# Bias table in one transfer, broadcast rows in stretches of 2 KB, and the last output bank in two halves

## The chip, the cores and the metric

The kernel runs on one core of a Trainium2 chip. The metric is the device time of one execution in microseconds (us), the median of several runs. The engines are named as in the profile: PE (matrix engine; PEld is its weight load, which runs beside the matmuls), DVE (vector), ACT (scalar), POOL, and SP, whose queue issues most of the transfers. ACT issues some as well. Each engine works through its own queue in order.

## The reference

A backbone of two layers over 256 latent tokens of width 2048, with 256 context tokens. Each layer begins with a modulated RMS norm; shift, scale and gate come from a conditioning vector by a matrix-vector product.

```python
for i in range(DEPTH):                       # DEPTH = 2
    shift, scale, gate = adaln(c, ada_w[i], ada_b[i])       # silu(c) @ w + b
    h = modulate(rms_norm(x, norm_g[i]), shift[:, None], scale[:, None])
    ...
    if i % 2 == 0:
        y, yc = na_ssd_mixer(h, hc, ...)     # 16 attention heads beside 32 SSD heads, then @ w_out
    else:
        y = short_conv_mixer(h, ...)         # four projections, a convolution of 3 taps, a gate, @ sc_w_out
    x = x + gate[:, None] * y
```

Two pieces of the first layer matter here. The attention of a latent row adds a bias, looked up in a small table for each head, to the scores of the latent keys, and masks the keys outside a window:

```python
s_lat = einsum('bqhd,bkhd->bhqk', qr, kb) * scale + bias      # bias = rpb[:, dr_idx, dc_idx]
s_lat = where(mask, s_lat, -inf)
s_ctx = einsum('bqhd,bkhd->bhqk', qr, k_ctx) * scale
pr = softmax(concatenate([s_lat, s_ctx]))
```

The SSD heads, in both directions of the sequence, use the running sum of dt * a along the sequence, and its exponential:

```python
cs = cumsum(dtc * a, axis=1)
decay = exp(where(tri, cs[:, :, None] - cs[:, None, :], -inf))
y = y + einsum('bign,bgrpn->bigrp', cc, h) * exp(cs)[..., None]
```

## The kernel before

All products with weights run in a form that keeps most of fp32: each operand is split into a high part and the rest, and three matmuls (high x high, high x low, low x high) add into one PSUM bank. A weight chunk of 512 KB is loaded by SP into one of five raw buffers; ACT casts it to the high part (line 422); DVE subtracts to get the low part (line 429); then PE uses both. The chunks go through in a fixed order (first layer's inputs, four groups of attention and SSD projections, w_out, then sc_in and sc_out of the second layer), and this stream sets the time line.

Everything else is written into the gaps by a planner. `Plan` holds a modelled clock for each engine and a modelled landing time for each transfer (`RATE`, 270 bytes a ns, line 42; lines 110 to 118). Small generators ("tasks") hold the side work. Between matmuls `pump` asks `may` for each task whether its next step is due on the modelled clocks, and if so writes it out there. So the order of instructions on each engine is fixed when the program is built, and a changed cost or condition in the plan can move other instructions. There are three lists of tasks: urgent, side and back; a task of the last is taken only when the first two have nothing due.

The tasks that the change touches:

- `gemv_gen` (line 872), the only task of the last list: the gate of the first layer and all of the second layer's modulation are 128 dot products on DVE, each of a loaded block of 128 x 1024 with the conditioning vector (line 885). Their loads (`adaT`) share the raw buffers with the weights: `issue` (line 367) loads the next block only when a buffer is free and enough weight chunks are already there. The results are asked for in three stages by `n_back` (lines 1725, 1762, 2103).
- `head_gen` (line 1134), one of 16 attention heads: it loads the head's bias into one of two bias tiles (line 1141), adds the mask to three pieces of it (line 1146), and later reads the tile as the bias of the 416 keys of each of two query blocks (line 1163). Between the pieces the tile holds zeros, set once by a memset (line 994), for the context keys.
- `dt_gen` (line 1264): it computes the running sums and writes them, and their exponentials, to DRAM as `csr` and `exr`, 64 rows of 256 (32 heads, twice for the two directions), by ACT's queue (lines 1352, 1353).
- `make_x` and `group_gen`: each head's two rows are read back, spread over 64 or 128 partitions, in stretches of 1 KB (lines 1482 and 1523).
- `fin_gen` (line 2101): the last step for each 512 output columns. It loads the gate's row, multiplies the bank with it on DVE (line 2112), adds the residual (line 2114) and sends the result out (line 2116). For the last 512 columns the final matmuls are ordered by rows of tokens: all that is left for the first 128 tokens (t = 0), then the same for the second (lines 2129 to 2139), so that the first half's end runs under the second half's matmuls.

Of the kernel before, what the change touches and what calls it, by code (L numbers as in the profile page):

```python
# [11 lines left out]
ALU = mybir.AluOpType  # L12
# [129 lines left out]
def kernel(ctx: ExitStack, tc, x, cx, ada0, w0, adaT, w_in, w_out, sc_in, sc_out, rpb, small, const,  # L142
# [9 lines left out]
    plan = Plan()  # L152
# [5 lines left out]
    def drt(shape, name):  # L158
        return dr.tile(list(shape), F32, name="dram_" + name)
# [35 lines left out]
    def mm(o, l, r, start, stop):  # L195
        E(T.matmul(o, l, r, start=start, stop=stop, skip_group_check=True))  # L196
# [143 lines left out]
    def give(pool, *bs):  # L340
        pool.extend(bs)
# [501 lines left out]
    def dot_gen():  # L843
# [8 lines left out]
        for j in DOTS:  # L852
# [17 lines left out]
            got.add(("S", j))  # L870

    def gemv_gen():
        yield from rows_out(csil, crow.rearrange("r (b c) -> (r b) c", c=128), 32)
        got.add("crow")
        yield when(lambda: ("S", DOTS[-1]) in got)
        for q, blocks in enumerate(GEM):
            for h in range(2):
                yield W_("SP", crow, csb)
                E(DMA.dma_start(csb, crow[0, h * 1024:(h + 1) * 1024].partition_broadcast(128)))
                for m in blocks:  # L880
                    yield when(lambda: ("gem", m, h) in RAW and plan.ready([RAW["gem", m, h][0]]) + 1500 <= plan.t["DVE"])
                    yield W_("DVE", RAW["gem", m, h][0], csb)
                    raw, _ = RAW.pop(("gem", m, h))
                    ngem[0] -= 1
                    E(V.tensor_tensor_reduce(out=raw, in0=raw, in1=csb, scale=1.0, scalar=0.0, op0=ALU.mult, op1=ALU.add,  # L885
                                             accum_out=gp[:, h, m:m + 1]))
                    give_raw(raw)
                    issue()
# [104 lines left out]
    for b_ in bias:  # L993
        E(G.memset(b_.rearrange("p a b -> p (a b)")[:, 128:544], 0.0))
    dcol = P_("dcol")
# [138 lines left out]
    def head_gen(a, h):  # L1134
# [3 lines left out]
        yield W_("SP")  # L1138
        bf = bt.rearrange("p a b -> p (a b)")[:, :672]
        for o_, c_, n_ in ((0, 0, 128), (304, 128, 64), (544, 192, 128)):  # L1140
            E(DMA.dma_start(bf[:, o_:o_ + n_], rpb[hd, :, c_:c_ + n_]))
        yield W_("DVE", bt)
        for o_, m_ in ((0, mask[:, 0:32]), (304, mid), (544, mask[:, 32:64])):
            n_ = m_.shape[-1]
            bv = bf[:, o_:o_ + 4 * n_].rearrange("p (c r) -> p c r", r=4)
            E(V.tensor_tensor(out=bv, in0=bv, in1=m_.unsqueeze(2).to_broadcast([128, n_, 4]), op=ALU.add))  # L1146
# [12 lines left out]
        def top(qt, ps):  # L1159
            sp = sps[qt] = tmp()  # L1160
            if qt == 0:
                E(V.memset(sp[:, 416:480], 0.0))
            b_ = bass.AP(tensor=bf.tensor, offset=bf[:, 336 * qt:].offset, ap=[bf.ap[0], [128, 2], [1, 208]])
            sc = sp[:, span(qt)]
# [96 lines left out]
    ncs, ebc = st([128, 2, 64], "ncs"), st([128, 64], "ebc")  # L1261
    csr, exr = drt([64, 256], "csr"), drt([64, 256], "exr")

    def dt_gen(ps):
# [86 lines left out]
        yield W_("AQ", rw)  # L1351
        E(DMA2.dma_start(csr, rw[:64, 0:256]))
        E(DMA2.dma_start(exr, rw[:64, 256:512]))
        give(free_t, rw)
# [63 lines left out]
    def make_x(s, gi, ps):  # L1418
# [11 lines left out]
        if True:  # L1430
# [45 lines left out]
            for b in range(2):  # L1476
# [3 lines left out]
                for hh in range(2):  # L1480
                    e0 = exr[4 * g + 2 * b + hh, :]
                    E(DMA.dma_start(two(Et)[64 * hh:64 * hh + 64],
                                    bass.AP(tensor=e0.tensor, offset=e0.offset, ap=[[0, 64], [32 * 256, 2], [1, 256]])))
                yield W_("PE", h1t, nb=1)
# [17 lines left out]
    def group_gen(s, gi):  # L1502
# [14 lines left out]
        for b in range(2):  # L1517
            yield W_("SP", csr)
            rows = []
            for hh in range(2):  # L1520
                rw = tmp()
                r0 = csr[4 * g + 2 * b + hh, :]
                E(DMA.dma_start(two(rw), bass.AP(tensor=r0.tensor, offset=r0.offset, ap=[[0, 128], [32 * 256, 2], [1, 256]])))
                rows.append(rw)
# [576 lines left out]
    def fin_gen(n, ps):  # L2101
        cols = slice(n * 512, (n + 1) * 512)
        yield when(lambda: n_back[0] >= 15)
        gb, o = tmp(), tmp()
        yield W_("SP", mrow[1:2])
        E(DMA.dma_start(gb, mrow[1, cols].partition_broadcast(128)))
        for t in range(2):
            if t:
                o = tmp()
            yield when(lambda: n < 3 or (3, t) in at)  # L2110
            yield W_("DVE", ps[t], gb)
            E(V.tensor_tensor(out=o, in0=ps[t], in1=gb, op=ALU.mult))
            give(free_b, ps[t])
            E(V.tensor_tensor(out=o, in0=o, in1=x1[t][:, cols], op=ALU.add))
            yield W_("SP", o)
            E(DMA.dma_start(out[t * 128:(t + 1) * 128, cols], o))
            give(free_t, o)
        give(free_t, gb)
# [10 lines left out]
    ws = [use(q) for q in range(3)]  # L2129
    for t in range(2):  # L2130
        for q, (H, Lo) in enumerate(ws):
            for b in range(2):
                hl = y2[KB - 6 + 2 * q + b]
                for a_, w_ in ((0, H), (0, Lo), (1, H)):
                    mm(ps[t], hl[:, a_, t * 128:(t + 1) * 128], w_[:, b], False, q == 2 and b == 1 and a_ == 1)
                pump()
        at.append((3, t))
        pump()
# [75 lines left out]
```

## Time and profile before

| | |
|---|---|
| median of 3 runs | 1743.96 us (1742.33 to 1747.86) |
| the profiled execution | 1743.12 us, its span in the trace 1741.3 us |
| matrix engine (PE) busy | 1718.7 us, 99% |
| DVE busy | 1251.3 us, 72% |
| ACT busy | 776.8 us, 45% |
| read from DRAM | 379.27 MB, 223 GB/s over the span |

The profile is one execution of the program, recorded by the hardware. "Busy" is the time in which an engine works on an instruction; matmuls overlap in a pipeline, so a busy PE is one that has at least one in flight. In rows of instructions stand the line of the code, the engine, the operation, the output and inputs by the program's names, their shapes, and how often. A bracket at the end gives the idle time of the engine just before, and what ended it. A row of transfers gives their size and the median time from issue to landing.

### The profile page before, as it was taken

The numbers are of one execution on the slowest core, as the hardware profiler recorded it, in microseconds if no ns is written. First come the engines' busy times: TensorE is split into PE (matmuls) and PEld (weight loads), VectorE is DVE, ScalarE is ACT, GpSimd is POOL, SyncE is SP. The second block draws the span as 40 slices with busy tenths as digits, with TensorE's granted clock in tenths as the row PEclk, the third lists the DMA queues.
The fourth block names the chain that finished last, engine by engine and source line by source line (L and its number), as shares of the span: only waits on it lengthen the run. The fifth ranks groups of instructions, "written<-read, shape, count | busy, mean of one in ns | idle before, by whom it ended". The sixth has DMA issues, their size and how long they took to land.

```text
span 1741.3 us, 24796 instructions
## 1 busy us (share of the span) xinstructions
PE 1718.7 (99%) x9237; PEld 1450.3 (83%) x9237; DVE 1251.3 (72%) x2106; ACT 776.8 (45%) x1367; POOL 33.9 (2%) x28
## 2 busy tenths in 40 slices
PE   6999999999999999999999999999999999999998
PEld 4777988888888889888888898888888888888887
DVE  5698788867575878475878587887667667676754
ACT  5434544445243445243435243665445344444442
POOL 0000100001000001000001000000000000000000
PEclk9999999999999999999999999999999999999999
DMA  9987644676654765654776567757867878787863
GB/s 360 373 325 271 206 134 150 195 210 195 201 170 140 229 205 180 205 170 139 229 208 199 177 196 235 249 195 258 292 209 246 280 258 266 263 282 257 286 214 113
DMA packets 198872, 390.52 MB, mean 224 GB/s; under 512 B 18712, under 2 KB 58456, under 8 KB 198496
## 3 DMA queue, kind: packets, MB, share of 16 engines
q1 hardware_dynamic: 191472, 382.35, 67.5%
q10 hardware_dynamic: 7280, 6.59, 1.1%
q8 instruction: 72, 1.18, 0.3%
q14 instruction: 48, 0.39, 0.1%
HBM read 379.27 MB, written 9.62 MB: 223 GB/s over the span
## 4 chain that ended last, share of the span: by engine, by line
PE 94%; DMA 3%; DVE 2%; ACT 0%; issue 0%; SPq 0%; POOL 0%; DVEq 0%; ACTq 0%
PE bank L196 91%; PE bank L200 3%; DMA raw<-in_ada 1%; DMA tmp<-dram_mixd 1%; DMA csb<-dram_crow 1%; DVE w L429 0%; DMA bias<-in_rpb 0%; DVE csb L859 0%; DVE raw L885 0%; DVE mix L1704 0%; DVE tmp L1547 0%; SPq L603 0%; SPq L383 0%; DVE raw L859 0%; DVE bias L1146 0%
## 5 line engine op out<-in xcount | busy, mean ns | idle before, releaser
L422 ACT CAST w<-raw 128x1024 fp32r<-128x1024 f32 (+1 forms) x344 | 360.0, 1048 | 550.2 <-PE bank L196 415.6
L429 DVE TENSOR_TENSOR w<-raw,w 128x1024 fp32r<-128x1024 f32 (+1 forms) x344 | 416.7, 1215 | 246.3 <-ACT w L422 244.0
L196 PE MATMUL bank<-hH,w 128*128 128x256 f32 (+1 forms) x2064 | 485.6, 324 | 1.3 <-DVE w L429 1.3
L196 PE MATMUL bank<-w,hH 128*128 128x512 f32 x1280 | 406.0, 396 | 3.3 <-ACT hH L780 2.5
L196 PEld LDWEIGHTS bank<-hH,w 128*128 128x128 f32 x2064 | 344.6, 188 | 33.9 <-DVE w L429 1.9
L196 PE MATMUL bank<-hL,w 128*128 128x256 f32 (+1 forms) x1040 | 334.3, 321 | 0.0
L196 PEld LDWEIGHTS bank<-w,hH 128*128 128x128 f32 x1280 | 238.1, 189 | 55.1 <-ACT hH L780 3.0
L196 PE MATMUL bank<-w,hL 128*128 128x512 f32 x640 | 249.9, 391 | 0.2
L196 PEld LDWEIGHTS bank<-hL,w 128*128 128x128 f32 x1040 | 196.4, 189 | 14.7
L196 PE MATMUL bank<-w,h 128*128 128x512 f32 x768 | 178.5, 389 | 0.0
L196 PEld LDWEIGHTS bank<-w,h 128*128 128x128 f32 x768 | 143.9, 188 | 29.8
L885 DVE CUSTOM_DVE_ANT_0 raw<-raw,csb 128x1024 f32<-128x1024 f32 x128 | 154.9, 1216 | 0.3 <-DMA csb<-dram_crow 0.3
L196 PEld LDWEIGHTS bank<-w,hL 128*128 128x128 f32 x640 | 120.4, 188 | 25.9 <-DVE hL L792 0.9
L196 PE MATMUL bank<-w,mix 128*128 128x512 f32 x588 | 138.7, 392 | 0.6 <-DVE w L429 0.4
L196 PEld LDWEIGHTS bank<-w,mix 128*128 128x128 f32 x588 | 109.4, 188 | 23.5 <-DVE w L429 0.8
L1367 DVE SCALAR_TENSOR_TENSOR tmp<-bank,cwh,tmp 128x508 f32<-128x508 f32 (+1 forms) x96 | 71.2, 745 | 1.9
L196 PE MATMUL bank<-KL,h 128*128 128x512 f32 x264 | 63.8, 389 | 0.0
L429 DVE TENSOR_TENSOR KL<-raw,KL 128x1024 fp32r<-128x1024 f32 x32 | 39.1, 1223 | 28.2 <-ACT KL L422 28.0
L196 PEld LDWEIGHTS bank<-KL,h 128*128 128x128 f32 x264 | 49.5, 188 | 10.2
L196 PE MATMUL bank<-QT,h 128*128 128x512 f32 x168 | 55.6, 390 | 0.0
L196 PE MATMUL bank<-wH,h 128*128 128x512 f32 x168 | 55.3, 389 | 0.0
L429 DVE TENSOR_TENSOR wL<-raw,wH 128x1024 fp32r<-128x1024 f32 x31 | 37.9, 1222 | 20.6 <-ACT wH L422 20.6
(306 smaller groups left out, 1956.1 us busy)
## 6 DMA issues: line engine op xcount, KB each, us to landing
raw<-in_w_in SPq DMA_DIRECT2D x196, 512.0 KB, 3.8
raw<-in_adaT SPq DMA_DIRECT2D x128, 512.0 KB, 4.8
raw<-in_sc_in SPq DMA_DIRECT2D x128, 512.0 KB, 5.0
raw<-in_w_out SPq DMA_DIRECT2D x64, 512.0 KB, 4.6
raw<-in_ada SPq DMA_DIRECT2D x35, 512.0 KB, 8.0
raw<-in_sc_out SPq DMA_DIRECT2D x32, 512.0 KB, 4.4
raw<-in_w SPq DMA_DIRECT2D x16, 512.0 KB, 5.6
tmp<-dram_csr SPq DMA_DIRECT2D x32, 256.0 KB, 6.3
```

The lines of the kernel that those rows point to most:

```text
L196: E(T.matmul(o, l, r, start=start, stop=stop, skip_group_check=True))
L200: E(T.transpose(o, i, ident if k == 128 else ident[:k, :k]))
L422: E(S.copy(H, v))
L429: E(V.tensor_tensor(out=Lo, in0=v, in1=H.bitcast(F32), op=ALU.subtract))
L885: E(V.tensor_tensor_reduce(out=raw, in0=raw, in1=csb, scale=1.0, scalar=0.0, op0=ALU.mult, op1=ALU.add, accum_out=gp[:, h, m:m + 1]))
L1367: E(V.scalar_tensor_tensor(out=do, in0=di, scalar=cwh[:, 32 * k + ch:32 * k + ch + 1], in1=do, op0=ALU.mult, op1=ALU.add))
```

## The change

1. The bias table on the host gets 64 columns of zeros, so that each head's bias is three equal pieces of 128 columns, and one transfer with a strided destination loads all three. The third piece moves from column 544 of the tile to column 608, the memset is 64 columns longer, and the second query block reads its bias in two stretches 192 columns apart.
2. `csr` and `exr` are laid out by head, with both directions of a head side by side. Four transfers write them instead of two; the reads spread one stretch of 2 KB instead of two of 1 KB.
3. The dot products of `gemv_gen` get a second condition: one may also be written out when fewer than (planned PE time / 9600 ns - 22) have been, whether or not its data is planned to be there 1.5 us before DVE comes to it.
4. The last 512 output columns of the second 128 tokens are finished in two halves of 256 columns: 18 matmuls of 256 columns, then another 18, each half followed by its own multiplication, addition and transfer.

```diff
+    n_dot = [0]
@@ gemv_gen
-                    yield when(lambda: ("gem", m, h) in RAW and plan.ready([RAW["gem", m, h][0]]) + 1500 <= plan.t["DVE"])
+                    yield when(lambda: ("gem", m, h) in RAW and (n_dot[0] < plan.t["PE"] / 9600.0 - 22 or plan.ready([RAW["gem", m, h][0]]) + 1500 <= plan.t["DVE"]))
...
+                    n_dot[0] += 1
@@ the memset of the bias tiles
-        E(G.memset(b_.rearrange("p a b -> p (a b)")[:, 128:544], 0.0))
+        E(G.memset(b_.rearrange("p a b -> p (a b)")[:, 128:608], 0.0))
@@ head_gen
-        bf = bt.rearrange("p a b -> p (a b)")[:, :672]
-        for o_, c_, n_ in ((0, 0, 128), (304, 128, 64), (544, 192, 128)):
-            E(DMA.dma_start(bf[:, o_:o_ + n_], rpb[hd, :, c_:c_ + n_]))
+        bf = bt.rearrange("p a b -> p (a b)")[:, :736]
+        E(DMA.dma_start(bass.AP(tensor=bf.tensor, offset=bf.offset, ap=[bf.ap[0], [304, 3], [1, 128]]), rpb[hd]))
         yield W_("DVE", bt)
-        for o_, m_ in ((0, mask[:, 0:32]), (304, mid), (544, mask[:, 32:64])):
+        for o_, m_ in ((0, mask[:, 0:32]), (304, mid), (608, mask[:, 32:64])):
...
-            b_ = bass.AP(tensor=bf.tensor, offset=bf[:, 336 * qt:].offset, ap=[bf.ap[0], [128, 2], [1, 208]])
+            b_ = bass.AP(tensor=bf.tensor, offset=bf[:, 336 * qt:].offset, ap=[bf.ap[0], [128 + 64 * qt, 2], [1, 208]])
@@ csr and exr
-    csr, exr = drt([64, 256], "csr"), drt([64, 256], "exr")
+    csr, exr = drt([32, 2, 256], "csr"), drt([32, 2, 256], "exr")
...
-        E(DMA2.dma_start(csr, rw[:64, 0:256]))
-        E(DMA2.dma_start(exr, rw[:64, 256:512]))
+        for d_ in range(2):
+            E(DMA2.dma_start(csr[:, d_, :], rw[32 * d_:32 * d_ + 32, 0:256]))
+        for d_ in range(2):
+            E(DMA2.dma_start(exr[:, d_, :], rw[32 * d_:32 * d_ + 32, 256:512]))
@@ make_x
-                    e0 = exr[4 * g + 2 * b + hh, :]
-                    E(DMA.dma_start(two(Et)[64 * hh:64 * hh + 64],
-                                    bass.AP(tensor=e0.tensor, offset=e0.offset, ap=[[0, 64], [32 * 256, 2], [1, 256]])))
+                    e0 = exr[4 * g + 2 * b + hh]
+                    E(DMA.dma_start(Et[64 * hh:64 * hh + 64], e0.rearrange("d t -> (d t)").partition_broadcast(64)))
@@ group_gen
-                r0 = csr[4 * g + 2 * b + hh, :]
-                E(DMA.dma_start(two(rw), bass.AP(tensor=r0.tensor, offset=r0.offset, ap=[[0, 128], [32 * 256, 2], [1, 256]])))
+                r0 = csr[4 * g + 2 * b + hh]
+                E(DMA.dma_start(rw, r0.rearrange("d t -> (d t)").partition_broadcast(128)))
@@ fin_gen
-        for t in range(2):
-            if t:
+        for t, c0, c1 in ((0, 0, 512), (1, 0, 512)) if n < 3 else ((0, 0, 512), (1, 0, 256), (1, 256, 512)):
+            if t and not c0:
                 o = tmp()
-            yield when(lambda: n < 3 or (3, t) in at)
-            yield W_("DVE", ps[t], gb)
-            E(V.tensor_tensor(out=o, in0=ps[t], in1=gb, op=ALU.mult))
-            give(free_b, ps[t])
-            E(V.tensor_tensor(out=o, in0=o, in1=x1[t][:, cols], op=ALU.add))
-            yield W_("SP", o)
-            E(DMA.dma_start(out[t * 128:(t + 1) * 128, cols], o))
-            give(free_t, o)
+            c = slice(c0, c1)
+            yield when(lambda: n < 3 or (3, t, c1) in at)
+            yield W_("DVE", ps[t][:, c], gb)
+            E(V.tensor_tensor(out=o[:, c], in0=ps[t][:, c], in1=gb[:, c], op=ALU.mult))
+            if c1 == 512:
+                give(free_b, ps[t])
+            E(V.tensor_tensor(out=o[:, c], in0=o[:, c], in1=x1[t][:, n * 512 + c0:n * 512 + c1], op=ALU.add))
+            yield W_("SP", o[:, c])
+            E(DMA.dma_start(out[t * 128:(t + 1) * 128, n * 512 + c0:n * 512 + c1], o[:, c]))
+            if c1 == 512:
+                give(free_t, o)
@@ the last matmuls
-    for t in range(2):
+    for t, c0, c1 in ((0, 0, 512), (1, 0, 256), (1, 256, 512)):
         for q, (H, Lo) in enumerate(ws):
             for b in range(2):
                 hl = y2[KB - 6 + 2 * q + b]
                 for a_, w_ in ((0, H), (0, Lo), (1, H)):
-                    mm(ps[t], hl[:, a_, t * 128:(t + 1) * 128], w_[:, b], False, q == 2 and b == 1 and a_ == 1)
+                    mm(ps[t][:, c0:c1], hl[:, a_, t * 128:(t + 1) * 128], w_[:, b, c0:c1], False, q == 2 and b == 1 and a_ == 1)
                 pump()
-        at.append((3, t))
+        at.append((3, t, c1))
         pump()
@@ host: the bias table
-    table = np.concatenate([pick(0, kc[:32]), pick(0, kc[32:40]), pick(1, kc[24:32]), pick(1, kc[32:])], axis=2)
+    table = np.concatenate([pick(0, kc[:32]), pick(0, kc[32:40]), pick(1, kc[24:32]), np.zeros((16, 128, 64), np.float32),
+                            pick(1, kc[32:])], axis=2).reshape(16, 128, 3, 128)
```

## The prediction

> **What bounds the kernel now.** I read the page's head, its busy times, then the busy time by stretches, then the few places where the matrix engine stands still.
>
> ```profile
> span 1741.3 us, 24796 instructions
> PE 1718.7 (99%) x9237; PEld 1450.3 (83%) x9237; DVE 1251.3 (72%) x2106; ACT 776.8 (45%) x1367; POOL 33.9 (2%) x28
> ...
> 0.00:211.00 211.00, 195.05 (x1259) 150.54 (x1260) 156.53 (x298) 101.61 (x216) 8.63 (x12) 0.99 0.85 310
> 211.00:403.00 192.00, 192.00 (x1126) 168.18 (x1125) 150.40 (x303) 90.85 (x194) 1.67 (x2) 1.00 0.58 175
> 403.00:406.00 3.00, 1.68 (x14) 1.35 (x12) 2.24 (x4) 3.00 (x11) 2.24 (x2) 1.00 0.50 141
> 406.00:1105.00 699.00, 699.00 (x3982) 608.04 (x3981) 503.77 (x905) 293.70 (x570) 18.36 (x10) 1.00 0.63 194
> 1105.00:1115.00 10.00, 9.42 (x40) 7.16 (x39) 9.90 (x24) 7.65 (x15) 0.00 (x0) 1.00 0.58 196
> 1115.00:1736.00 621.00, 621.00 (x2825) 514.94 (x2825) 427.06 (x574) 279.95 (x364) 3.02 (x4) 1.00 0.75 247
> 1736.00:1741.30 5.30, 0.51 (x3) 0.08 (x1) 1.38 (x2) 0.00 (x0) 0.00 (x0) 0.98 0.13 49
> ```
>
> PE is the bound: 1718.7 of 1741.3 us, at a granted clock of 1.00 almost throughout. The windows (stretch, length, busy time of PE, PEld, DVE, ACT and POOL with instructions, granted clock, DMA share, GB/s) say where the other 22.6 us lie: 15.95 before 211 us, 1.32 at 403 to 406, 0.58 at 1105 to 1115, 4.79 after the last matmul, and none anywhere else. The change removes no matmul work. Before 211 us it alters only the length of one memset, since the first heads' bias loads begin at 219.7 us (row below) and the new condition for the dot products is false up to 22 x 9.6 = 211 us of planned PE time. So there are 1.32 + 0.58 = 1.90 us of standstill to win in the body, and something of the tail. Anything beyond must be lost, not won.
>
> **Part 1, the bias in one transfer.** The 1.32 us is the one place where the bias loads set PE's pace:
>
> ```profile
> 394.02 4.86 SPq L1141 DMA_DIRECT2D bias<-in_rpb  x6
> 401.60 1.21 DVE L1146 TENSOR_TENSOR bias<-bias,const 128x128 f32<-128x128 f32 x6 [1.04 <-DMA bias<-in_rpb]
> 402.80 1.22 DVE L885 CUSTOM_DVE_ANT_0 raw<-raw,csb 128x1024 f32<-128x1024 f32 x1
> 403.94 1.22 DVE L429 TENSOR_TENSOR w<-raw,w 128x1024 fp32r<-128x1024 f32 x1
> 402.21 1.12 ACT L422 CAST w<-raw 128x1024 fp32r<-128x1024 f32 x1
> 405.21 0.50 PE L196 MATMUL bank<-hH,w 128*128 128x256 f32 x2 [1.32 <-DVE w L429]
> ...
> L1141 SPq DMA_DIRECT2D bias<-in_rpb x48: 384/430/1962, 219.7 to 1146.2; - x48
> ```
>
> Two heads issue six bias transfers, 4.86 us on SP's queue. DVE stands 1.04 us for the last, then does six mask additions, one dot product (402.80) and the low half of a weight (403.94), and PE waits for that one. Two issues instead of six take four issues of 0.43 us, 1.7 us, off SP, so DVE's 1.04 us would go. But the weight's low half also needs ACT's cast, which ends at 402.21 + 1.12 = 403.33. It can move from 403.94 to 403.35 at the earliest, so PE wins **0.6**, not 1.04. Ends: 1.3 won (the cast moves too), 0 won (the order changes and the stall stays). The other fourteen heads win nothing: PE had no wait there. The bytes of a head grow from 320 to 384 columns on 128 partitions, 160 to 192 KB, and the mask additions all wait for the one transfer; elsewhere DVE's 503.77 of 699 us covers that. The 256-byte stretches go; no other row tells what that alone is worth, and PE's full windows hide it. The two memsets grow by 64 of 416 columns at 444 ns, 0.07 us each, on an idle POOL.
>
> **Part 2, rows in stretches of 2 KB.**
>
> ```profile
> tmp<-dram_csr SPq DMA_DIRECT2D x32, 256.0 KB, 6.3
> tmp<-dram_mrow SPq DMA_DIRECT2D x12, 256.0 KB, 4.9
> ACT tmp L1532 <- DMA tmp<-dram_csr: 18.6, 10, 3.2
> L1352 ACTq DMA_DIRECT2D dram_csr<-tmp x1: 507/507/507, 260.3 to 260.3; - x1
> ```
>
> The same bytes are read in half as many pieces. The nearest row is the spread of mrow, 256 KB in stretches of 2 KB, at 4.9 us against 6.3. ACT's 18.6 us of waiting for these rows may shrink by up to 10 x 1.4 us. PE stands nowhere behind it (full windows), so its price is **0**; ends: 0 and the 0.58 us counted in part 3. If the cover went, each late row would cost its 1.4 us. Writing takes four issues on ACT's queue instead of two, once: about 2 x 0.5 = 1 us near 260 us, behind which weight casts wait, with ACT busy 90.85 of 192 us: 0.
>
> **Part 3, the pacing of the dot products.** The diff also lets a dot product of the conditioning (1.22 us on DVE, 128 of them) be written out when fewer than t/9.6 - 22 have been, without the old demand that its data lie planned 1.5 us ahead of DVE.
>
> ```profile
> 150.00:700.00 550.00, 56.08 (x92) 1.00 0.60 186
> 700.00:1000.00 300.00, 41.09 (x68) 1.00 0.61 189
> 1000.00:1200.00 200.00, 15.83 (x26) 1.00 0.71 228
> 1200.00:1440.00 240.00, 20.76 (x34) 1.00 0.76 253
> 1440.00:1650.00 210.00, 22.06 (x36) 1.00 0.82 272
> ...
> L885 DVE CUSTOM_DVE_ANT_0 raw<-raw,csb x128: 1149/1217/1224, 168.5 to 1645.2; 128x1024 f32<-128x1024 f32 x128
> raw<-in_adaT SPq DMA_DIRECT2D x128, 512.0 KB, 4.8
> ```
>
> A dot is two instructions, so before has done 46, 80, 93, 110 and 128 of them at the ends of these windows (stretch, length, DVE's busy time in them with its instructions, clock, DMA). The line asks for 51, 82, 103 and 128 at 700, 1000, 1200 and 1440 us. It is ahead of before throughout, so the new condition bites. DVE is given 18 x 1.3 = 23 us of work earlier, all before 1440 us, and as much less after; totals stay. The new clause only opens where the plan has DVE behind PE. Nothing waits for the earlier results: the code asks for the last of them only before the outputs of the last projection, and the last dot started at 1645.2 us. What is added is a wait: a dot whose data is late holds DVE's queue, with the next weight's low half behind it, and PE behind that. The plan reckons such a load at 1.0 + 1.94 + 1.0 = 3.9 us (lines 42, 115 and 116: 512 KB at 270 bytes a ns between two constants of 1 us); the row says 4.8. The 1.5 us covered that 0.9 and goes.
>
> The trace has no stall of this kind, but it has the same queue: the dot at 402.80 stands ahead of the weight at 403.94, and PE lost 1.32. All positions after 219 us shift by a little besides, since the plan's SP clock is charged two issues less for each head. Ends: 0.58 won (the second standstill also goes) and six stalls of 1.3, 7.8 lost. I take **+1.0**, one stall between the two sizes seen (0.58 and 1.32): a plan with just two standstills in 1500 us has more ways to gain one than to lose one.
>
> **Part 4, the tail in two halves.**
>
> ```profile
> 1732.26 1.52 PE L196 MATMUL bank<-KL,y 128*128 128x512 f32 x6
> 1736.12 0.39 PE L196 MATMUL bank<-wH,y 128*128 128x512 f32 x1
> 1736.54 0.69 DVE L2112 TENSOR_TENSOR tmp<-bank,tmp 128x512 f32<-128x512 f32 x1 [2.66 <-PE bank L196]
> 1737.27 0.69 DVE L2114 TENSOR_TENSOR tmp<-tmp,x1b 128x512 f32<-128x512 f32 x1
> out<-tmp SPq DMA_DIRECT2D x8, 256.0 KB, 2.3
> dram_mixd<-half ACTq DMA_DIRECT2D x24, 128.0 KB, 2.1
> ```
>
> ```profile
> 229.25 0.39 PE L196 MATMUL bank<-hH,w 128*128 128x256 f32 x2
> 229.59 0.39 PE L196 MATMUL bank<-hH,w 128*128 128x256 f32 x2
> L1571 DVE TENSOR_TENSOR half<-bank,yi x16: 408/416/425, 393.5 to 1160.3; 128x256 f32<-128x256 f32 x16
> 14.46 3.53 DVE L649 COPY xm<-bank 128x256 f32<-128x256 f32 x8 [1.48 <-ACT xm L648]
> ```
>
> The last 18 matmuls start from 1732.26 to 1736.12, 0.227 us apart. Three of 256 columns with their own weight loads take 0.34 us (229.25 to 229.59), 0.113 each, so 36 cost the same PE time as 18. DVE's last two operations fall from 0.69 each to about the 0.42 of line 1571 (at 512 columns the one on the bank and the one on tiles take the same), the last matmul's run-out from 0.39 to 0.39 - 0.11 = 0.28: 0.54 + 0.11 = 0.65 off. The last transfer halves; by the 2.1 us of the 128 KB rows that is 0.2 off. Together **-0.85** if the halves run freely.
>
> They may not. The multiplication of the first half is written out before the second half's matmuls, and both use one bank. The copy at line 649 reads the upper half of a bank into its own tile and still waits 1.48 us for ACT's copy of the lower half: users of one bank are kept apart here, whatever the columns. Then PE waits: the first half's last matmul starts at 1732.26 + 17 x 0.113 = 1734.18 and ends at 1734.46, DVE reads 1734.49 to 1734.91, PE resumes at 1734.96 (0.05 us from release to start, as from 403.94 + 1.22 to 405.21) and ends at 1737.16, and DVE at 1738.06 instead of 1737.96. So 0.1 lost, 0.2 won by the smaller transfer: **-0.1**. Behind the waiting matmul stand only the other 17 of its half; DVE's last two operations and the last transfer wait for them. Ends: -0.85 (no wait), +0.1 (the transfer no faster).
>
> [...]
>
> **Sum.** The profiled execution took 1743.12 us (span 1741.3). 1743.12 - 0.6 + 0 + 1.0 - 0.1 = **1743.4**. It lies 0.84 under the median of before, 1743.96, whose runs go from 1742.33 to 1747.86; 0.3% of it (5.2 us) is about what a measurement can tell from no change, so the forecast is: no change.
>
> **The rivals.**
> - *The halves run freely*: the tail gives 0.85 instead of 0.1, 1742.6. For it: the columns are disjoint, and the accumulation is one group. Against: line 649. Still within 0.3%. Chance 0.14.
> - *The pacing doesn't do what it says*: a dot's load waits for a free buffer and for four waiting weights, so the loads may set the pace and not the condition; the order stays, 1743.12 - 0.6 - 0.1 = 1742.4. For it: only 17 dots in 1200 to 1440 us, at a DMA share of 0.76. Against: 80 by 1000 us under the same rule. Chance 0.13.
> - *Slower: early dots block DVE.* Place: 211 to 1440 us, where DVE is 72 to 78% busy (150.40 of 192, 503.77 of 699). With a median of 4.8 us more than half of the loads land later than planned; if one in twenty of some 120 dots meets a weight that PE already wants, that is six stalls of 1.3 us: 1743.4 - 1.0 + 7.8 = 1750.2. It decides from six on: five give 1748.9, still within 0.3% of 1743.96 (1749.2). For it: the 402.80 sequence. Against: PE's full windows show that weights usually have room to spare. Chance 0.25.
> - *Faster by over 0.3%*: under 1738.7. All standstill of the body and the best tail give 1743.12 - 1.9 - 0.85 = 1740.4, so only scatter gets there. Chance 0.03.
>
> The forecast has the remaining 0.45. **Range:** 1740.4 rounded down to 1740 below; above, the six stalls and a median as far over the profile as before's (0.84): 1751.5. Its own range, and that of the first two rivals, is 1740.4 to 1746 (two more stalls of 1.3 over the forecast). Faster 0.03, within 0.3% 0.45 + 0.14 + 0.13 = 0.72, slower 0.25.
>
> **What would show it.** Part 1: two bias issues where there were six, PE's 1.32 us near 404 us down to about 0.7. Part 2: transfers of csr near 4.9 us, PE's windows still full. Part 3: the last dot near 1440 us; waits of line 885 for in_adaT, absent before, would be the slower rival, and only if PE waits for line 429 behind them. Part 4: 36 matmuls of 256 columns, a gap of about 0.5 us on PE between the halves, DVE ending 1.5 us after the last matmul's start. The prediction is wrong if PE stands more than 5 us in the body, or if PE's busy time grows.

## The result, and the profile after

| | before | after |
|---|---|---|
| median (range, runs) | 1743.96 us (1742.33 to 1747.86, 9) | 1740.13 us (1739.29 to 1741.80, 9) |
| ratio, 95% interval | | 0.9977 (0.9968 to 0.9986) |
| profiled execution, its span | 1743.12, 1741.3 us | 1740.13, 1738.3 us |
| PE busy | 1718.7 us | 1717.7 us |

The change wins 0.23%, and the interval leaves no doubt that it is a win. The medians differ by 3.8 us, the two profiled executions by 3.0; the profile of before, 1743.12, lies 0.84 under the median of its kernel. The 3.0 us are what the traces can explain. Compared at the same matmul, the changed kernel is 0.18 us ahead of before at 254 us and 2.88 ahead at 1724 us, so 2.7 us are won in the body and 0.1 in the tail.

The page's head of the changed kernel and its busy time by stretches (stretch, length, busy time of PE, PEld, DVE, ACT and POOL with instructions, granted clock, DMA share, GB/s):

```profile
span 1738.3 us, 24820 instructions
...
0.00:211.00 211.00, 194.57 (x1262) 149.69 (x1262) 157.01 (x298) 101.61 (x216) 8.74 (x12) 1.00 0.86 310
...
403.00:406.00 3.00, 3.00 (x28) 3.00 (x27) 2.27 (x5) 1.47 (x4) 0.61 (x1) 1.00 0.95 293
406.00:1105.00 699.00, 699.00 (x3973) 607.89 (x3972) 517.64 (x930) 294.64 (x570) 17.70 (x10) 1.00 0.65 204
1105.00:1115.00 10.00, 10.00 (x46) 8.35 (x45) 8.73 (x21) 6.97 (x14) 0.00 (x0) 1.00 0.79 273
1115.00:1733.00 618.00, 617.48 (x2820) 512.77 (x2819) 414.15 (x550) 277.34 (x361) 3.83 (x4) 1.00 0.73 237
...
```

Both standstills of the body are gone: 3.00 of 3.00 us at 403 to 406, 10.00 of 10.00 at 1105 to 1115. Before 211 us PE is idle 16.4 us against 16.0, nothing won there. The 0.52 us missing after 1115 us are the new gap in the tail, shown below.

How much a standstill costs is not what the idle column says. PE's time line of before, around the first one (start, length, instruction):

```profile
403.08 0.28 PE L196 MATMUL bank<-hL,w 128*128 128x256 f32 x1
403.19 0.58 PE L196 MATMUL bank<-hH,w 128*128 128x256 f32 x2
403.62 0.28 PE L196 MATMUL bank<-hL,w 128*128 128x256 f32 x1
405.21 0.50 PE L196 MATMUL bank<-hH,w 128*128 128x256 f32 x2 [1.32 <-DVE w L429]
```

Matmuls of this form started about 0.117 us apart just before (402.02 to 402.72, six steps). Here one starts 405.21 - 403.62 = 1.59 us after its predecessor, 1.47 too late; of the 1.59 us, the 0.28 that the predecessor runs count as busy. The two at 403.19 took 0.43 us to 403.62 instead of 0.23. Together that is 1.67 us lost, for 1.32 us idle.

### The profile page after: what moved, and what is told of

Same layout as the page of the kernel before. It is cut to its first block, busy times and chain, and to the rows that moved or that the text cites. A ratio compares the mean times of both kernels' runs of the same rounds, so it can differ in the third digit from the quotient of the medians.

```text
span 1738.3 us, 24820 instructions
## 1 busy us (share of the span) xinstructions
PE 1717.7 (99%) x9255; PEld 1451.5 (84%) x9255; DVE 1253.3 (72%) x2108; ACT 776.2 (45%) x1367; POOL 33.2 (2%) x28
## 4 chain that ended last, share of the span: by engine, by line
PE 96%; DMA 2%; DVE 2%; issue 0%; SPq 0%; ACT 0%; POOL 0%; DVEq 0%; ACTq 0%
PE bank L196 93%; PE bank L200 3%; DMA raw<-in_ada 1%; DMA full<-dram_crow 1%; DVE csb L859 0%; DVE w L429 0%; DVE raw L859 0%; SPq L603 0%; DVE gt L818 0%; DVE yi L859 0%; DVE tmp L623 0%; DVE hL L792 0%; DVE sz L818 0%; DVE tmp L2116 0%; SPq L383 0%
## 5 line engine op out<-in xcount | busy, mean ns | idle before, releaser
L429 DVE TENSOR_TENSOR QL<-raw,QT 128x1024 fp32r<-128x1024 f32 x32 | 39.1, 1223 | 22.1 <-ACT QT L422 21.8
```

Of the source, the lines that this page charges most:

```text
L429: E(V.tensor_tensor(out=Lo, in0=v, in1=H.bitcast(F32), op=ALU.subtract))
```

## The experiments

Twelve kernels were run. First the parts alone, then the parts taken out, then the mechanism. The ratio is to runs of before taken beside the run on the same chip; "idle" is PE's, from the busy time in the stretches 403 to 410 and 1105 to 1135 us (before: 1.32 and 0.58).

| run | median, us (range, runs) | ratio to before (95%) | idle |
|---|---|---|---|
| e1: bias, order of before | 1747.18 (1745.05 to 1749.95, 11) | 1.0008 (0.9999 to 1.0017) | 2.05, 1.08 |
| e2: bias alone | 1746.38 (1743.97 to 1749.28, 11) | 1.0006 (0.9997 to 1.0014) | 2.37, 0.91 |
| e3: pacing alone | 1751.31 (1750.52 to 1754.85, 5) | 1.0037 (1.0023 to 1.0051) | 5.45, 0.43 |
| e4: tail alone | 1744.91 (1743.89 to 1745.76, 11) | 0.9996 (0.9987 to 1.0005) | 1.05, 0.62 |
| e5: rows, order of before | 1740.26 (1739.58 to 1743.08, 11) | 0.9974 (0.9965 to 0.9983) | 0, 0 |
| e6: all but the bias | 1740.10 (1739.06 to 1741.54, 10) | 0.9975 (0.9966 to 0.9984) | 0, 0 |
| e7: all but the rows | 1751.62 (1751.00 to 1754.40, 5) | 1.0045 (1.0032 to 1.0058) | 5.80, 0.43 |
| e8: all, another order at the end | 1739.21 (1738.57 to 1740.32, 7) | 0.9970 (0.9959 to 0.9981) | 0, 0 |
| e9: rows of 512 bytes | 1802.05 (1798.98 to 1805.05, 4) | 1.0326 (1.0309 to 1.0344) | many |
| e10: csr alone | 1740.81 (1740.13 to 1741.78, 9) | 0.9977 (0.9967 to 0.9987) | 0, 0 |
| e11: rows, order of before, end of e8 | 1740.53 (1738.37 to 1741.51, 7) | 0.9972 (0.9962 to 0.9983) | 0, 0 |
| e12: 1 KB rows, each from its own place | 1741.23 (1740.00 to 1742.80, 9) | 0.9982 (0.9972 to 0.9992) | 0, 0 |

A part changes the plan's modelled clocks, and with them the order of all work. Where a run says "order of before", the plan is charged as in before, so that PE, DVE and ACT carry the same instructions in the same order and only transfers differ.

**e1, the bias in one transfer, nothing else moved.** Before with the diff's lines for the bias, and the plan's clocks set back behind them:

```diff
+        d0, w0_, r0_ = plan.dma, dict(plan.w), dict(plan.r)
         E(DMA.dma_start(bass.AP(tensor=bf.tensor, offset=bf.offset, ap=[bf.ap[0], [304, 3], [1, 128]]), rpb[hd]))
+        s_, plan.dma = plan.t["SP"] - 450, d0
+        for u_, n_ in (((0,), 65536), ((2,), 32768), ((4, 5), 65536)):
...
+        plan.t["SP"] = s_
```

> The kernel before with the bias in one transfer, and with the plan's clocks charged as for three, so that matrix engine, DVE and ACT get exactly the order of before; only the bias transfers differ. If the transfer itself removed the standstill near 404 us (1.48 us from start to start of the two matmuls beyond the usual step), that gap falls to 0.9 or less and the span by 0.6 to 1.5 us; if the order did it, the gap stays at 1.3 to 1.5. The two gaps near 1107 and 1112 us (0.31 and 0.59) stay under both. In time: 0.9992 to 0.9997 of before for the first theory, 1.000 for the second.

The standstill near 404 us grew, which neither theory had. SP's bias issues at that place (line, count, nanoseconds smallest/median/largest, first and last start; then who waits):

```profile
L1149 SPq DMA_DIRECT2D bias<-in_rpb x2: 597/1620/2642, 394.3 to 395.0; - x2
...
  DVE bias L1163: 1.7, 1
```

There are two issues instead of six, but one of them took 2.64 us, and DVE waited 1.7 us instead of 1.0. So fewer issues did not bring the bias in earlier: one issue on SP's queue was held. This run does not show what held it; e5 changes the transfers ahead of it.

**e2, the bias alone**, with the plan's new clocks (the diff's own lines).

> The kernel before with the bias in one transfer, the plan charged as the changed code charges it (20 rows of the matrix engine's order move). If the bias is the cause near 404 us: the gap gone, 1.5 us less, 1107 and 1112 us as before. If the pacing or the layout of the rows is: all three gaps there, within 0.3 us of before.

The same picture with a little reordering: 2.37 us idle at one place, 1.0006 of before. The bias part alone wins nothing.

**e3, the pacing alone** (the diff's lines that count the dot products go with it).

```diff
-  yield when(lambda: ("gem", m, h) in RAW and plan.ready([RAW["gem", m, h][0]]) + 1500 <= plan.t["DVE"])
+  yield when(lambda: ("gem", m, h) in RAW and (n_dot[0] < plan.t["PE"] / 9600.0 - 22 or plan.ready([RAW["gem", m, h][0]]) + 1500 <= plan.t["DVE"]))
```

> The kernel before with only the new condition for the dot products. If earlier dots take DVE's load off the stretch near 1105 us: the gaps at 1107 and 1112 us (0.9 together, 1.1 with the slow steps behind them) go, the one at 404 stays or moves, 1 us less. If they block DVE, as the slower rival has it: DVE waits for in_adaT at the dots' line, and new gaps of 1.3 us on the matrix engine, slower than before.

6.1 us slower than the median of before beside it (1745.21). DVE's time line, and PE's clock by stretches:

```profile
404.90 0.66 DVE L1149 TENSOR_TENSOR bias<-bias,const 128x128 f32<-128x128 f32 x3 [6.12 <-DMA bias<-in_rpb]
406.15 0.63 DVE L1149 TENSOR_TENSOR bias<-bias,const 128x128 f32<-128x128 f32 x3 [0.58 <-DMA bias<-in_rpb]
```

```profile
410.00:420.00 10.00, 10.00 (x67) 10.00 (x67) 7.77 (x13) 3.85 (x6) 1.89 (x1) 0.73 0.72 250
```

DVE stands 6.1 us for the bias, not for a dot product's data. PE then stands 5.45 us and afterwards runs at a granted clock of 0.73 for 10 us: another 2.7 us, an estimate from 10 x (1 - 0.73). The bias goes out at 398.4 us, 4.4 us later than in before, and lands after 5.6 to 6.5 us instead of 4.0 to 4.6. Ahead of it on SP's queue stand two csr transfers (394.2 and 394.6 us), a dot product's load (396.8) and a weight chunk (397.9). Which of them delays it, this run alone does not show; the changed kernel has the same sequence with rows of 2 KB, sends the bias at 391.5 us and has no such wait.

**e4, the tail alone.**

> The kernel before with only the last bank in two halves; the order is that of before up to the last 18 matmuls. Bank wait: the matrix engine stands 0.5 us between the halves, DVE ends 6.1 to 6.2 us after the first matmul of the second 128 tokens (5.70 in before), the span falls by 0.0 to 0.3. Free halves: no gap, 0.85 less. In time 1.000 under both, within the interval.

0.9996 of before with the order of the body untouched, and a gap of 0.52 us between the halves. Its standstill near 404 us was 1.05 us where before had 1.32: the same order gave somewhat different waits in two executions.

**e5, the rows in 2 KB, nothing else moved.** The parts so far leave only the rows. Before with the layout `[32, 2, 256]` of csr and exr, written and read as in the diff, and the plan charged for one transfer each as in before:

```diff
+        for o_, c_ in ((csr, 0), (exr, 256)):
+            for d_ in range(2):
+                E(DMA2.dma_start(o_[:, d_, :], rw[32 * d_:32 * d_ + 32, c_:c_ + 256]))
...
-                E(DMA.dma_start(two(rw), bass.AP(tensor=r0.tensor, offset=r0.offset, ap=[[0, 128], [32 * 256, 2], [1, 256]])))
+                E(DMA.dma_start(rw, r0.rearrange("d t -> (d t)").partition_broadcast(128)))
```

(The rows alone in the plan's own new order were not run.)

> Before with the rows of csr and exr in stretches of 2 KB and nothing else changed; the planned clocks are charged as before, so that PE, DVE and ACT keep the order of before. Theory A (the two csr transfers of 1 KB stretches, issued at 392 us and 5.7 to 7.8 us under way, back up the transfers behind them, so that the bias lands late and DVE, then PE, stand): the csr transfers near 392 us take 4.2 to 5.2 us, the bias issues behind them take 0.4 to 0.6 us each instead of one of 2 us, DVE waits less than 0.3 us for the bias near 400 us, PE's standstill of 1.05 to 1.32 us near 404 us is gone, and the time is 1.0 to 1.5 us under before. Rival B (the stall belongs to the order, in which a dot product stands ahead of a weight's low half; the length of the stretches is worth nothing, as the prediction had it): the standstill near 404 us stays at 1.0 to 1.3 us, and the time is that of before within 0.5 us.

The whole of the win is here: 0.9974, with before's order, three bias transfers a head, no pacing and the old tail. The medians differ by 4.8 us, more than the 1.0 to 1.5 that theory A gave; the two traces, below, by 2.8. The transfers near 392 us and the bias behind them, first in before, then in e5:

```profile
L1523 SPq DMA_DIRECT2D tmp<-dram_csr x2: 421/440/460, 392.0 to 392.4; - x2
...
DMA to landing us min/median/max: 5.7/6.7/7.8
...
L1141 SPq DMA_DIRECT2D bias<-in_rpb x6: 423/430/1962, 394.0 to 398.5; - x6
```

```profile
L1534 SPq DMA_DIRECT2D tmp<-dram_csr x2: 418/420/422, 390.7 to 391.2; - x2
...
DMA to landing us min/median/max: 4.8/4.9/5.0
...
L1141 SPq DMA_DIRECT2D bias<-in_rpb x6: 328/427/438, 392.8 to 395.5; - x6
```

The two rows land in 4.8 to 5.0 us instead of 5.7 to 7.8, none of the six bias issues takes over 0.44 us, and DVE's mask additions no longer wait. The second standstill has the same root on ACT's queue. Before's mix tiles issued at 1086 to 1093 us, and ACT's cast that waits for one; then e5's:

```profile
L1698 ACTq DMA_DIRECT2D tmp<-dram_mixd x5: 367/378/1637, 1085.9 to 1092.7; - x5
...
DMA to landing us min/median/max: 4.6/7.3/10.1
```

```profile
1102.99 0.41 ACT L1702 CAST mix<-tmp 128x256 fp32r<-128x256 f32 x1 [1.69 <-DMA tmp<-dram_mixd]
```

```profile
L1709 ACTq DMA_DIRECT2D tmp<-dram_mixd x6: 366/366/463, 1084.9 to 1097.4; - x6
...
DMA to landing us min/median/max: 3.5/4.0/5.9
```

Two csr transfers go out at 1089.6 and 1090.1 us in before and take 6.6 and 10.0 us; the mix tile issued behind them takes 10.1, and one issue is held for 1.64 us. In e5 nothing of the kind is left.

The order being the same in all 9237 matmuls, the same matmul can be found in both. Before, then e5:

```profile
389.42 0.39 PE L196 MATMUL bank<-w,hL 128*128 128x512 f32 x1
...
1102.87 0.35 PE L196 MATMUL bank<-KT,QT 128*128 128x416 f32 x1
...
1732.26 1.52 PE L196 MATMUL bank<-KL,y 128*128 128x512 f32 x6
```

```profile
389.55 0.39 PE L196 MATMUL bank<-w,hL 128*128 128x512 f32 x1
...
1101.37 0.35 PE L196 MATMUL bank<-KT,QT 128*128 128x416 f32 x1
...
1729.59 1.52 PE L196 MATMUL bank<-KL,y 128*128 128x512 f32 x6
```

e5 is 0.13 us behind at 389 us, 1.50 ahead at 1102 and 2.67 ahead at the end: 1.63 us won from the first to the second of them, across the standstill near 404 us, 1.17 from the second to the third, across the one near 1109 us, 2.80 in all, where the idle column had shown 1.90.

**e6, the change without the bias part** (three transfers of 320 columns again; rows, pacing and tail stay).

> The changed kernel with the bias again in three transfers a head of 320 columns (rows, pacing and tail stay). Theory A (rows in 2 KB remove the backlog; one bias transfer of 192 KB gives nothing): no standstill over 0.3 us near 404 us, time 1739.5 to 1740.5 us, as the changed kernel or a little under it. Rival B (the prediction's part 1: two issues instead of six take away DVE's wait for the bias): DVE waits about 1 us for the bias near 400 us again, PE stands 0.6 to 1.3 us at 403 to 406 us, time 1740.7 to 1741.5 us.

1740.10 against the changed kernel's 1740.13, no standstill. With the rows in 2 KB the bias is in time either way; the one transfer for the bias is worth nothing.

**e7, the change without the rows** (stretches of 1 KB again).

> The changed kernel with the rows of csr and exr again in stretches of 1 KB (bias, pacing and tail stay). Theory A: the csr transfers issued shortly before the bias of a pair of heads take 5.5 us or more again, the bias behind them lands late, DVE waits 1 to 6 us for it and PE stands 1 to 5 us near 400 to 406 us: time 1741.5 to 1750 us. Rival B (the bias in one transfer together with the pacing's order removes the standstill, the length of the stretches is worth nothing): no standstill near 404 us, time 1739.5 to 1740.7 us.

Slower by 0.45%, a little more than theory A's range. PE stands 5.83 us near 403 us and 1.25 us more in the 695 us from 410 us on, and the first engine to stand is DVE:

```profile
404.56 1.23 DVE L888 CUSTOM_DVE_ANT_0 raw<-raw,csb 128x1024 f32<-128x1024 f32 x1 [5.64 <-DMA raw<-in_adaT]
...
406.42 1.19 DVE L1148 TENSOR_TENSOR bias<-bias,const 128x128 f32<-128x128 f32 x6 [0.62 <-DMA bias<-in_rpb]
```

A dot product written out early stands at the head of DVE's queue while its data, behind the csr rows, is late: this is the prediction's slower rival, once, with a price of 5.8 us instead of six times 1.3. The rows in 2 KB take it away.

**e8, another order of the last matmuls**, on the changed kernel, so that PE never writes the bank that DVE reads:

```diff
...
-    for t, c0, c1 in ((0, 0, 512), (1, 0, 256), (1, 256, 512)):
+    for t, c0, c1 in ((1, 0, 256), (0, 0, 512), (1, 256, 512)):
```

The multiplications, additions and transfers at the end follow in the same order.

> The changed kernel with the last matmuls in another order: first the left half of the columns of the second 128 tokens, then all columns of the first 128 tokens, then the right half of the second, so that DVE reads the left half while PE writes into another bank. If PE's 0.5 us gap between the halves is the wait for a bank that DVE still reads: the gap is gone, the last matmul starts 0.5 us earlier, and the time is 0.4 to 0.7 us under the changed kernel (1739.4 to 1739.7 us). If the gap comes from something else (the weights' load for the new half, the issue of the matmul behind the wait): a gap of 0.3 us or more stays ahead of the last half, and the time is that of the changed kernel within 0.2 us.

The gap is gone. PE's and DVE's time line of the changed kernel between its two halves, then PE's of e8 at the start of the last half:

```profile
1731.41 0.28 PE L196 MATMUL bank<-wH,y 128*128 128x256 f32 x1
...
1731.73 0.42 DVE L2116 TENSOR_TENSOR tmp<-bank,tmp 128x256 f32<-128x256 f32 x1 [0.73 <-PE bank L196]
...
1732.21 0.98 PE L196 MATMUL bank<-KL,y 128*128 128x256 f32 x6 [0.52 <-DVE tmp L2116]
```

```profile
1725.72 0.88 PE L196 MATMUL bank<-KL,y 128*128 128x256 f32 x6
...
1731.75 0.39 PE L196 MATMUL bank<-wH,y 128*128 128x512 f32 x1
1731.98 0.88 PE L196 MATMUL bank<-KL,y 128*128 128x256 f32 x6
```

1731.98 follows 1731.75 at the usual 0.23 us. From the first of these last matmuls to the end of the span e8 takes 1737.9 - 1725.72 = 12.2 us; the changed kernel took 13.0 (from 1725.30) and before 13.1 (from 1728.18). The median, 1739.21, is 0.9 us under that of the changed kernel and a little under the 1739.4 that was expected at best; but the two kernels were not measured beside each other and the intervals of the ratios overlap, so it is the trace that shows the 0.8.

**e9, rows of 512 bytes.** Is it the number of stretches, or did e5 just shift a few transfers by luck? Before with `csr, exr = drt([2, 2, 32, 128])`, so that each row is read in four stretches, in before's order:

```diff
...
+                E(DMA.dma_start(rw.rearrange("p (k t) -> p k t", k=4), bass.AP(tensor=r0.tensor, offset=r0.offset, ap=[[0, 128], [4096, 4], [1, 128]])))
```

> Before with the rows of csr and exr in stretches of 512 bytes, twice as many as in before, for the same bytes; PE, DVE and ACT keep the order of before. Theory A (the number of stretches decides how long a row transfer is under way and how far what stands behind it is held): the csr transfers near 392 us take longer than the 5.7 and 7.8 us of before, DVE waits 2 us or more for the bias, PE's standstill near 404 us grows from 1.05-1.32 us to 2 us or more, and the time is 2 us or more over before. Rival B (the 1.75 us near 404 us and the 1.2 us near 1109 us of the run with 2 KB stretches came from a chance shift in time of a few transfers, not from the stretches): csr as in before, a standstill near 404 us of 0 to 1.3 us, time within 1.5 us of before.

57 us slower. It is no longer the bias alone: at 392 us PE stands 9.63 us for what ACT and DVE make of the rows themselves. The csr transfers' median, which was 6.3 us in before and 5.0 in e5, and the DMA between 407 and 410 us, when all packets that run are of 512 bytes:

```profile
tmp<-dram_csr SPq DMA_DIRECT2D x32, 256.0 KB, 12.9
```

```profile
DMA  5333022112151263121816048121212214213110
...
DMA packets 245, 0.13 MB, mean 42 GB/s; under 512 B 0, under 2 KB 245, under 8 KB 245
...
q1 hardware_dynamic: 245, 0.13, 29.1%
```

245 stretches in 3 us, 82 a microsecond, with the DMA engines busy 29% of the time (last line; the first gives it in tenths, in 40 slices). So the engines have time to spare; what they wait for is not shown.

**e10, csr alone in 2 KB, exr as before.**

> Before with the rows of csr alone in stretches of 2 KB and exr in stretches of 1 KB; PE, DVE and ACT keep the order of before. Theory A (the two csr transfers, 256 KB each, hold the bias at 394 us and the mix tiles at 1091 us): both standstills gone, time 1739.9 to 1740.9 us, that of the run with both rows changed. Rival B (exr, 128 KB a piece, has a share): a standstill of 0.5 us or more stays at one of the two places, time 1741.2 us or more.

1740.81 and no standstill: csr carries the effect, exr (128 KB, half of a csr transfer) adds nothing that shows.

**e11, e5 with e8's end**: neither the bias part nor the pacing.

> Before with the rows of csr and exr in stretches of 2 KB and the last matmuls in the order left half of the second 128 tokens, first 128 tokens, right half; no bias change, no pacing. Theory A (bias and pacing give nothing for time): no standstill near 404 and 1109 us, no gap ahead of the last half, time 1738.9 to 1739.7 us, as the changed kernel with the same order of the last matmuls. Rival B (the pacing or the one bias transfer gives something of its own): 0.5 us or more over that, 1739.8 us or more.

The median, 1740.53, is over theory A's range and in rival B's; but its runs reach from 1738.37 to 1741.51, so the time doesn't tell it from e8. The trace does: PE never stands from 211 us on, and the last stretch is e8's (1739.2 - 1726.99 = 12.2 us). The difference lies before 211 us, where none of the changes acts:

```profile
0.00:100.00 100.00, 85.33 (x602) 61.45 (x603) 62.31 (x143) 51.20 (x102) 3.18 (x10) 0.98 0.94 358
100.00:211.00 111.00, 108.53 (x642) 87.22 (x641) 92.38 (x153) 49.87 (x113) 5.46 (x2) 1.00 0.78 266
```

PE is idle 17.1 us there against 16.4 in the changed kernel, and the clock of the first 100 us is 0.98. At the same matmul e11 is 1.12 us behind e8 at 200 us and 1.28 behind at 1724 us. So of the 1.3 us only 0.2 arise where the bias and the pacing act, and the rival is refuted by the trace: with the rows in 2 KB the two are worth 0.2 us at most. (e6, which has the pacing and not the bias, keeps step with e8 from 254 us to the tail to 0.03 us.)

**e12, 1 KB stretches, each partition from its own place.** In before all 128 partitions read the same two stretches. Here each reads its own rows of the weights; the bytes, the 256 stretches of 1 KB and the order stay. The rows' values are left out, and with them the right output; one subtraction becomes an addition:

```diff
-                r0 = csr[4 * g + 2 * b + hh, :]
-                E(DMA.dma_start(two(rw), bass.AP(tensor=r0.tensor, offset=r0.offset, ap=[[0, 128], [32 * 256, 2], [1, 256]])))
+                r0 = w_in[128 * (4 * (g % 4) + 2 * b + hh):, 0:1024]
+                E(DMA.dma_start(two(rw), bass.AP(tensor=r0.tensor, offset=r0.offset, ap=[[r0.ap[0][0], 128], [512, 2], [1, 256]])))
...
-                                             op0=ALU.subtract, op1=ALU.min))
+                                             op0=ALU.add, op1=ALU.min))
```

> Before, with the csr transfers still in 256 stretches of 1 KB, but each partition reads its own row of the weights in DRAM instead of all 128 reading the same two rows; the rows' values are left out (DVE's subtraction of csl becomes an addition, so that the exponentials stay finite), the rest is computed on. PE, DVE and ACT keep the order of before. Theory A1 (what is slow is many stretches read from one place): the csr transfers near 392 us land in 5 us or less, the bias issues behind them take 0.6 us or less each, no standstill over 0.3 us near 404 and 1109 us, time 1740 to 1741.5 us. Theory A2 (the number of stretches is slow wherever they are read from): csr 5.7 to 7.8 us, one bias issue of 1 us or more, a standstill of 1.0 us or more near 404 us and 0.4 us or more near 1109 us, time that of before within 0.7 us.

The time fell to 1741.23 and both standstills are gone. The DMA while these rows run in e12 (394 to 395.5 us) and the rows' median landing there, then the DMA in before (394.5 to 397.5):

```profile
DMA packets 552, 0.59 MB, mean 396 GB/s; under 512 B 38, under 2 KB 520, under 8 KB 552
```

```profile
tmp<-in_w_in SPq DMA_DIRECT2D x32, 256.0 KB, 4.5
```

```profile
DMA packets 431, 0.49 MB, mean 165 GB/s; under 512 B 30, under 2 KB 397, under 8 KB 431
```

368 packets a microsecond against 144, and 4.5 us to landing against 6.3. Counted by their size, the 512 packets of 1 KB of these two transfers start within 2.1 us in e12 and within 5.7 us (394.1 to 399.8) in before, 90 a microsecond, about as many as the 82 of half that size in e9. So in these runs it isn't short stretches as such: it is many stretches out of one place, and there their number counted more than their length. (The weights also differ from csr in that the kernel didn't write them; that csr lies in freshly written scratch wasn't separated from its being one place.)

## Why the prediction was wrong, and where it was right

It forecast no change, 1743.4 us, with 0.72 on "within 0.3%". 1740.13 lies within 0.3% and, by 0.1 us, inside the range of 1740.0 to 1751.5; but the win is real, and the sum had its terms in the wrong places. That it lies in the range is luck: the lower end is 1740.4 rounded down, and the 1740.4 rests on a bound that was too small. Neither of the signs of being wrong that the prediction gave could catch this: PE does not stand in the body at all, and its busy time is 1717.7 us.

- **Part 1 (-0.6): wrong step.** "Two issues instead of six take four issues of 0.43 us, 1.7 us, off SP, so DVE's 1.04 us would go." The bias wasn't late for the number of its issues. Alone it cost 1.1 us of idle PE at 404 us (e2: 2.37 against 1.32), 1.4 by the starts of the same matmul; left out it costs nothing (e6). The sign was in a row that the prediction quoted: of 48 bias issues the median took 0.43 us and the largest 1.96, and the largest was one of the six at 394 us. What stood ahead of the held issue was csr; with csr in 2 KB none of these issues took over 0.44 us (e5).
- **Part 2 (0): the failed step that decides.** "PE stands nowhere behind it (full windows), so its price is 0". PE stood behind the rows at both of its standstills, through the bias on SP's queue and the mix tiles on ACT's. The windows were full everywhere else, and the two that were not were put down to the engine or transfer that was last in the chain. The landing time itself was well judged: 4.9 us from the mrow row, 5.2 measured. It won 2.8 us (e5).
- **Part 3 (+1.0): wrong for the changed kernel, and far too small alone.** In the changed kernel PE stands nowhere behind line 888, though DVE does wait there as the slower rival said:

```profile
L888 DVE CUSTOM_DVE_ANT_0 raw<-raw,csb x128: 1149/1218/1227, 168.1 to 1508.2; 128x1024 f32<-128x1024 f32 x128
...
  DMA raw<-in_adaT: 9.1, 9
```

  Nine waits, 9.1 us together, all covered. The last dot starts at 1508 us rather than near 1440, against 1645 before. With 1 KB rows the same pacing costs 6 to 7 us (e3, e7). Costing the parts one at a time and adding could not have given this: part 3's price depends on part 2.
- **Part 4 (-0.1): right.** From the first matmul of the second 128 tokens to the end of the span: 1738.3 - 1729.38 = 8.92 us against 1741.3 - 1732.26 = 9.04, so 0.1 won. PE waited for the bank with a gap of 0.52 us where about 0.5 was forecast; that the halves run freely is refuted, for PE and DVE too. Inside it the sizes were off both ways: DVE ended 6.17 us after that start rather than 5.80, and the last transfer and what follows won 0.6 rather than 0.2; that the two cancel is luck.
- **The bound of 1.90 us in the body: mis-sized.** It was read from PE's idle time; the two places cost 2.80 us (e5), since at the first of them the 0.28 us that the last matmul ahead of it ran count as busy, and the two before that took 0.43 us instead of 0.23. With 2.8 and the 0.1 of the tail, and nothing for parts 1 and 3, the sum would have been 1743.12 - 2.9 = 1740.2; measured 1740.13.
- **"Faster by over 0.3%", 0.03**, rested on that bound: all standstill and the best tail gave 1740.4. The changed kernel and the best one tried (e8, 1739.21) are both under that, and over the 1738.7 from which the case begins.
- **Two slips of arithmetic** change nothing: 1750.2 + 0.84 is 1751.0 and not 1751.5, and the prediction's own times put DVE's end 1738.06 - 1736.88 = 1.2 us after the last matmul's start and not 1.5; measured 1735.55 - 1734.34 = 1.2.

## What to carry to other kernels

Where an engine waits for a transfer, look at what was issued ahead of it, on its own queue and on the other one, before counting its own issues: the longest issue of a group (1.96 us beside 0.43) and the longest landing (10.1 beside 3.7) marked the spot. Rows that are spread over all partitions should lie in DRAM so that each partition takes one long stretch; here halving the number of stretches won 2.8 of the 3.0 us, while changing the waiting transfer or the order around it won nothing or lost. And a loss in PE's time is measured between the starts of the same matmul in two traces, not from the idle column.

## What the runs showed of the hardware

- **Stretches out of one place.** 128 partitions reading the same rows moved 42 GB/s in stretches of 512 bytes (e9) and 165 in stretches of 1 KB (before); from separate places stretches of 1 KB moved 396 (e12). The last two include the other packets of their windows. For rows that all partitions share, stretches of both sizes went at about the same pace, 82 a microsecond (e9) and 90 (before). What inside the memory or the DMA sets it, no run here shows, nor what exactly holds an issue on SP's queue (up to 2.64 us in e1, 4.3 in e9):

```profile
L1141 SPq DMA_DIRECT2D bias<-in_rpb x6: 430/856/4317, 406.1 to 415.6; - x6
```

- **The granted clock after a standstill.** In e3, where PE stood for 5.45 us between 403 and 410 us, the clock was 0.90 in those 7 us, 0.73 from 410 to 420 us and 1.00 from 420 to 440; in e7 (5.80 us) it was 0.77, 0.82 and 1.00. In e3 that comes on top of the standstill, by the estimate above with another 2.7 us. In e9 the clock was 0.79 from 392 to 425 us, where PE stood 15.45 of 33 us, and PE's busy time over the whole span was 1737.6 us against 1718.7 in before. After shorter ones it went either way: 1.00 from 400 to 420 us in e2 (2.37 us idle), but 0.84 from 403 to 410 us in e1 (2.05) and 0.94 over the next 10:

```profile
410.00:420.00 10.00, 10.00 (x84) 10.00 (x83) 9.04 (x15) 5.90 (x9) 0.00 (x0) 0.94 0.73 228
```

  What sets e1 apart from e2, the runs don't show.
- **Where the runs of one kernel differ.** From 254 us to the last matmul, traces of the same order without a standstill keep step: e5, e10 and e12 to 0.3 us, the changed kernel and e8 (up to the tail) to 0.5. The stretch before 211 us, at a DMA share of 0.86, varies by up to 2.0 us (the changed kernel and e11, at the same matmul near 200 us). That before's runs scatter more (5.5 us against 2.5) may come from its two standstills: the first was 1.32 us in before and 1.05 in e4, in the same order.
